# Expert parts above 128 rows: held weights in two passes of 256 middle columns, with a row count per rank

## The chip, the cores and the metric

The kernel runs on one core of a Trainium2 chip. The metric is the device time of one execution in microseconds, from the first to the last instruction of the core. A profile of one execution shows, for every engine, when each instruction ran and what it waited for.

## What is computed

The kernel is one layer of a diffusion backbone on 2048 latent tokens of 1024 channels, after 256 context tokens: an input projection, two groups of scans, an output projection with a norm, a mixture of experts, and a second norm. The change is in the mixture of experts, which the reference computes so (cut):

```python
weights = g_val * jax.nn.softmax(e_val, axis=-1)      # top group, then the two best of its 8 experts
expert_id = g_idx * EXPERTS_PER_GROUP + e_idx          # 32 experts, 2 for each of 2048 tokens
...
def expert_block(args):
    xb, e = args
    hid = jax.nn.silu(xb @ w1[e]) * (xb @ w3[e])       # 1024 -> 512 middle columns
    return hid @ w2[e]                                 # 512 -> 1024
...
return jnp.zeros((T, D), y.dtype).at[sorted_tok].add(y_slots)
```

All numbers are float32. On TensorE each product of two float32 matrices is made of three products of parts in the single-pass type float32r: high by high, low by high, and high by low.

## The kernel before

The projection, the scans, the first norm and the routing come first. The routing writes, for each expert, a list of token rows and weights (`idxD`), and takes the expert that leads in tokens as the first. Then the experts go by rank (by falling number of tokens). A fixed table, `NFIX`, says how many blocks of 128 rows each rank has: 3 for the first, 2 for the next 13, 1 for the last 18, 47 blocks together. A loop at the end (over `otab`) takes what the table did not foresee. The ranks with several blocks alternate with those of one (`sched`).

An expert's weights come in 12 pieces of 512 KB: 8 of `w1` and `w3`, each two chunks of 128 input channels by 512 middle columns, and 4 of `w2`. SyncE's queue fetches them in the order `pieces`, `NRAW` ahead. `split` makes of each raw piece a high part on ScalarE (`whi`) and a low part on VectorE (`wlo`), in a ring of `NUP` places for the way up and `NDOWN` for the way down. `pump` issues the next splits wherever the ring allows it.

A block goes through these steps. `gather` loads its list and its token rows with an indirect DMA. `turn` transposes the rows on TensorE and splits them into `xh`, `xl`. `up` multiplies: the 128 turned tokens are the stationary operand, 512 columns of weights move, and the result `ph` has a token on each partition. `hidden` makes SiLU and product. `turn_hidden` transposes the result and splits it into `hh`, `hl`. `down` multiplies them with `w2` (24 matmuls of 512 columns), and `put` scales the result and adds it to the tokens' rows in memory with an indirect DMA. The heart of `up` and of `down`:

```python
pe.matmul(p, self.xh[:, k, :], wh[:, kk, :], start=k == 0, stop=False)
pe.matmul(p, self.xl[:, k, :], wh[:, kk, :], start=False, stop=False)
pe.matmul(p, self.xh[:, k, :], wl[:, kk, :], start=False, stop=k == KC - 1)
...
pe.matmul(p, self.hh[:, k, :], wh[:, nh, :], start=k == 0, stop=False)
```

The program's order is written out by hand: for block `t` four steps of `up` (`kp`), and between them the turning of block `t + 1`, the transposes of the hidden values of block `t - 1` (after step 0), its way down (after step 1), and the gather for block `t + 2`. Every engine works through its own instructions in this order.

Of the kernel before, what the change touches and what calls it, by code (L numbers as in the profile page):

```python
# [19 lines left out]
D = 1024  # L20
# [13 lines left out]
NFIX = [3] + [2] * 13 + [1] * 18  # L34
NSB = sum(NFIX)
NOV = 30
NRAW, NUP, NDOWN = 10, 9, 4
# [4 lines left out]
# a word for each block of columns: the k chunk at which the scan is stepped, the steps there and after the block, and the  # L42
# order of what follows it: e evacuation, f filler, a scan steps, l later
# [28 lines left out]
def hymba_kernel(ctx, tc, xT, ctxT, x, small, rows, ada_w, w_in, gate_w, w_out, router_w, w1, w3, w2, out):  # L72
# [12 lines left out]
    u2D = dram.tile([L + 128, D], F32, name="u2D")  # L85
    accD = dram.tile([L + 128, D], F32, name="accD")
    idxD = dram.tile([32 * L, 2], I32, name="idxD")
# [30 lines left out]
    # ---- constants of the channels: forget-gate floor, decay rate of the RG-LRU  # L118
# [9 lines left out]
    def channel_constants():  # L128
# [11 lines left out]
        # softplus(-lam) = max(-lam, 0) + log1p(y), y = exp(-|lam|); log1p(y) = 2 artanh(y / (2 + y))  # L140
# [17 lines left out]
    def level_masks():  # L158
        """Level b pairs tokens of one 2b-block that lie in different b-halves."""
# [23 lines left out]
    # fixed blocks of a rank, rank on partition  # L183
# [3 lines left out]
    for v in range(max(NFIX)):  # L187
        pool.tensor_scalar(nmore, ecol, float(sum(n > v for n in NFIX)), None, op0=ALU.is_lt)
        pool.tensor_add(nfix, nfix, nmore)
    tok = const.tile([128, NTILE, 2, 2], I32, name="tok")  # L190
# [5 lines left out]
    # the expert of the first block, that block's rows, the expert of every rank, and the rank of every expert  # L196
# [5 lines left out]
    # every slot starts as a row past the tokens with weight 0, so that a block may be part full  # L202
    blank = tmp.tile([128, 512], I32, name="blank", tag="macc", bufs=1)
    zi = blank[:, 0:256].rearrange("p (r o) -> p r o", o=2)
    pool.memset(zi, 0)
    pool.iota(zi[:, :, 0], pattern=[[1, 128]], base=L, channel_multiplier=0)
    zero = blank[:, 256:512].bitcast(F32)
    pool.memset(zero, 0.0)

    def init_tables():  # L210
        rows0 = zero[:, None, :].to_broadcast([128, 4, 256])
        for a in range(4):
            pool.dma_start(idxD.rearrange("(p a r) o -> a p (r o)", p=128, a=4)[a], zi.rearrange("p r o -> p (r o)"))
            # rows past the tokens, and those of the last tile: the first block is read before that is stored
            if a < 3:
                t, r0 = ((u2D, L), (accD, L), (u2D, 0))[a]
                pool.dma_start(t[r0:r0 + 128, :].rearrange("p (n c) -> p n c", n=4), rows0)
            yield
# [4 lines left out]
    # ---- adaLN: shift and scale of the first layer norm, channel on partition  # L223
# [25 lines left out]
    def fetch_u(p, bi, k, n, pl, tag, bufs):  # L249
        """Raw channels of n chunks from chunk k."""  # L250
# [18 lines left out]
    def mod_sum(n0, also=()):  # L269
        """Columns n0 .. n0 + 3 on TensorE; also: k chunks of columns 4 .. 7 for VectorE meanwhile."""  # L270
# [53 lines left out]
    def build_u(p, bi, raws):  # L324
        """u = x * (1 + scale) + shift, channel on partition, split in two float32r; block bi of pass p, a chunk a step."""
# [53 lines left out]
    # ---- HGRN2  # L379
# [4 lines left out]
    class Head:  # L384
        """Head h over the W columns of pass p, the context first in pass 0."""
# [45 lines left out]
        def run(self):  # L431
            """The scan, in steps: every yield lets a block of the projection onto TensorE."""
# [65 lines left out]
            def chain(d, U, order):  # L498
                """States before each chunk of order; the state after the last goes to S."""
# [54 lines left out]
    # ---- RG-LRU  # L554
# [3 lines left out]
    class Lru:  # L558
        """Channels 128 t of the RG-LRU over the W columns of pass p."""
# [34 lines left out]
        def steps(self):  # L594
            """From the gates to the states of the first direction; rr: tanh, then sqrt(1 - a * a)."""
# [46 lines left out]
        def close(self):  # L642
            """Steps after the gates of the output are there: the other direction, or its store for later."""
# [15 lines left out]
    # the projection in blocks of columns, with the scans of the head before between them  # L659
# [62 lines left out]
    # at the turn of a pass the first blocks of two units go before their second ones, so that u can be made meanwhile  # L722
# [15 lines left out]
    # w_out takes the place of u when that is used up  # L738
# [131 lines left out]
    # ---- output projection, first norm, router, dispatch  # L870
# [5 lines left out]
    def rstd_of(pl, var, n, scale, eng=dve):  # L876
        """1 / sqrt(var * scale + EPS), elementwise on [128, n]."""
# [5 lines left out]
    with ExitStack() as st:  # L883
# [147 lines left out]
        def top2(i):  # L1031
# [22 lines left out]
            # the experts of the other groups are out  # L1054
# [9 lines left out]
            # weights: g_val * softmax of the two logits about their maximum  # L1064
# [22 lines left out]
        def place(i):  # L1087
# [7 lines left out]
            dve.scalar_tensor_tensor(dest[:, i, :], ee, float(L), sl, op0=ALU.mult, op1=ALU.add)  # L1095
# [172 lines left out]
    with ExitStack() as st:  # L1268
# [17 lines left out]
        def fetch(e, n, q=sp):  # L1286
            raw = er.tile([128, 2, 512], F32, name="raw", tag="raw")
            q.dma_start(raw, piece_src(e, n))
            return raw
# [305 lines left out]
```

## Time and profile before

| what | value |
|---|---|
| median of 3 runs (lowest to highest) | 2313.64 us (2311.78 to 2314.38) |
| the profiled execution: span of its instructions | 2313.6 us |
| first expert matmul to the end of the last way down | 1388.9 to 2238 us |
| busy in the span: TensorE, VectorE, ScalarE | 2125.5, 1758.1, 1165.0 us |
| moved by DMA | 446.01 MB |

The span of the profiled execution is its own time, and it agrees with the median. The busy time of TensorE is a sum of spans in which some matmul is under way; matmuls overlap, so the rate of a run of matmuls is read from their starts.

### The profile page before, as it was taken

To read this page: it belongs to the slowest core of one execution; us is meant where nothing else is said; L and a number is where in the kernel's file an instruction comes from. 1 tells how busy PE (TensorE), PEld (TensorE's weight loads), DVE (VectorE), ACT (ScalarE), POOL (GpSimd) and SP (SyncE) were. 2 spreads that over 40 slices of the span, in tenths; PEclk is the share of its full clock that TensorE was granted. 3 is DMA by queue.
4 is the path that set the end of the run, shared out by engine and by line. 5 is a ranking of instruction groups with operands and counts; after the bars stand their busy time and mean duration, and the time that the engine had idled before them with its cause. 6 is when DMAs were issued, how large, how long until landed. Compare 5 with 4: busy or idle time off the path is not lost.

```text
span 2313.6 us, 31918 instructions
## 1 busy us (share of the span) xinstructions
PE 2125.5 (92%) x11192; PEld 1824.8 (79%) x11192; DVE 1758.1 (76%) x2611; ACT 1165.0 (50%) x1807; POOL 609.4 (26%) x495
## 2 busy tenths in 40 slices
PE   7999999999999999996989969999999999999970
PEld 3788788999988988995777757888888888888850
DVE  5677776776776898896888975777777777777959
ACT  3446554654554654553333314555555555555733
POOL 4222233223233130002555551111111111111116
PEclk9999999999999999997999979999999999999985
DMA  8223243313424334328455228899999999999965
GB/s 266 96 99 114 78 146 101 123 62 121 136 77 139 101 107 139 126 95 293 148 172 171 88 80 292 285 298 299 302 299 299 301 298 289 288 295 294 355 194 242
DMA packets 213030, 446.01 MB, mean 193 GB/s; under 512 B 27635, under 2 KB 69619, under 8 KB 212356
## 3 DMA queue, kind: packets, MB, share of 16 engines
q1 hardware_dynamic: 186276, 378.37, 47.4%
q0 software_dynamic: 16784, 58.24, 10.2%
q10 hardware_dynamic: 9808, 7.34, 1.0%
q8 instruction: 89, 1.46, 0.3%
q14 instruction: 73, 0.60, 0.1%
HBM read 361.00 MB, written 82.89 MB: 192 GB/s over the span
## 4 chain that ended last, share of the span: by engine, by line
PE 64%; DVE 15%; issue 10%; DMA 5%; ACT 4%; POOL 2%; SPq 0%; POOLq 0%; DVEq 0%; ACTq 0%
PE ph L1337 7%; PE ph L1339 7%; PE ph L1338 7%; PE pp L349 7%; PE pp L351 7%; PE pp L350 7%; PE pye L1361 4%; PE pye L1363 4%; PE pye L1362 4%; PE pa L467 3%; PE pg L591 2%; DVE fr L987 2%; PE ptx L1325 2%; DMA raw<-in_w_dram 1%; POOL ur L340 1%
## 5 line engine op out<-in xcount | busy, mean ns | idle before, releaser
L1296 DVE TENSOR_TENSOR wlo<-raw,whi 128x1024 fp32r<-128x1024 f32 x384 | 455.2, 1222 | 81.9 <-ACT whi L1295 68.1
L349 PE MATMUL pp<-uh,wh 128*128 128x384 f32 (+2 forms) x1248 | 446.3, 358 | 4.6 <-ACT wh L239 2.4
L1295 ACT CAST whi<-raw 128x1024 fp32r<-128x1024 f32 x384 | 388.8, 1052 | 92.8 <-PE pye L1362 55.3
L350 PE MATMUL pp<-ul,wh 128*128 128x384 f32 (+2 forms) x1248 | 429.6, 344 | 4.8 <-DVE ul L240 4.8
L351 PE MATMUL pp<-uh,wl 128*128 128x384 f32 (+2 forms) x1248 | 428.6, 343 | 3.7 <-DVE wl L240 3.5
L1337 PE MATMUL ph<-whi,xh 128*128 128x512 f32 x752 | 309.1, 411 | 5.6 <-DMA raw<-in_w_dram 5.6
L1339 PE MATMUL ph<-wlo,xh 128*128 128x512 f32 x752 | 296.9, 395 | 2.2 <-DVE wlo L1296 2.2
L1338 PE MATMUL ph<-whi,xl 128*128 128x512 f32 x752 | 293.6, 390 | 0.0
L349 PEld LDWEIGHTS pp<-uh,wh 128*128 128x128 f32 x1248 | 239.4, 192 | 25.5 <-ACT rgs L592 5.2
L350 PEld LDWEIGHTS pp<-ul,wh 128*128 128x128 f32 x1248 | 239.0, 192 | 19.6 <-DVE ul L240 9.8
L351 PEld LDWEIGHTS pp<-uh,wl 128*128 128x128 f32 x1248 | 238.4, 191 | 13.9 <-DVE wl L240 4.9
L1308 POOL DMA_INDIRECT X<-u2D,ix x46 | 52.6, 1144 | 658.8 <-DMA ix<-idxD 565.8
L368 POOL TENSOR_SCALAR mraw<-mraw,sil 128x512 f32<-128x512 f32 x56 | 101.4, 1811 | 363.6 <-DMA mraw<-in_ada_w_dram 363.6
L1339 PEld LDWEIGHTS ph<-wlo,xh 128*128 128x128 f32 x752 | 141.6, 188 | 38.4 <-DVE wlo L1296 5.8
L1326 ACT CAST xh<-ptx 128x512 fp32r<-128x512 f32 x92 | 53.9, 586 | 226.3 <-PE ptx L1325 176.9
L1337 PEld LDWEIGHTS ph<-whi,xh 128*128 128x128 f32 x752 | 142.1, 189 | 30.3 <-ACT whi L1295 6.6
L1338 PEld LDWEIGHTS ph<-whi,xl 128*128 128x128 f32 x752 | 142.3, 189 | 25.8
L1361 PE MATMUL pye<-whi,hh 128*128 128x512 f32 x376 | 148.1, 394 | 0.7 <-ACT hh L1352 0.7
L1363 PE MATMUL pye<-wlo,hh 128*128 128x512 f32 x376 | 147.4, 392 | 0.0
L1362 PE MATMUL pye<-whi,hl 128*128 128x512 f32 x376 | 146.1, 389 | 0.2 <-DVE hl L1353 0.2
L467 PE MATMUL pa<-Q,km 128*128 128x128 f32 x896 | 124.9, 289 | 17.7 <-DVE Q L470 14.4
L240 DVE TENSOR_TENSOR wl<-wr,wh 128x1024 fp32r<-128x1024 f32 x84 | 108.5, 1292 | 39.1 <-ACT wh L239 39.1
(337 smaller groups left out, 4126.3 us busy)
## 6 DMA issues: line engine op xcount, KB each, us to landing
raw<-in_w_dram SPq DMA_DIRECT2D x384, 512.0 KB
wr<-in_w_in_dram SPq DMA_DIRECT2D x84, 512.0 KB
mraw<-in_ada_w_dram SPq DMA_DIRECT2D x64, 256.0 KB
aw<-in_ada_w_dram SPq DMA_DIRECT2D x16, 512.0 KB
fx<-in_x_dram SPq DMA_DIRECT2D x16, 512.0 KB
accD<-fr SPq DMA_DIRECT2D x16, 512.0 KB
u2D<-fu SPq DMA_DIRECT2D x16, 512.0 KB
f<-accD SPq DMA_DIRECT2D x16, 512.0 KB
```

The costliest lines, as they stand in the source:

```text
L349: pe.matmul(ps, wh[:, k, :], uh[:, k, :], start=k == 0, stop=False)
L350: pe.matmul(ps, wh[:, k, :], ul[:, k, :], start=False, stop=False)
L351: pe.matmul(ps, wl[:, k, :], uh[:, k, :], start=False, stop=k == KC - 1)
L467: pe.matmul(pa[:, c, :], km[:, s:s + 128], cut(Q, s, [(2 * b, 64 // b), (T + b, 2), (1, b)]), start=True, stop=True)
L1295: act.copy(hi, raw)
L1296: dve.tensor_sub(lo, raw, hi.bitcast(F32))
L1337: pe.matmul(p, self.xh[:, k, :], wh[:, kk, :], start=k == 0, stop=False)
L1338: pe.matmul(p, self.xl[:, k, :], wh[:, kk, :], start=False, stop=False)
L1339: pe.matmul(p, self.xh[:, k, :], wl[:, kk, :], start=False, stop=k == KC - 1)
L1361: pe.matmul(p, self.hh[:, k, :], wh[:, nh, :], start=k == 0, stop=False)
L1362: pe.matmul(p, self.hl[:, k, :], wh[:, nh, :], start=False, stop=False)
L1363: pe.matmul(p, self.hh[:, k, :], wl[:, nh, :], start=False, stop=k == 3)
```

## The change

Ranks get their own number of rows, `ROWS` (288 for the first, 224, 176, 160, 144 for the other thirteen above 128, then 128 down to 80), 4416 rows instead of 47 times 128 = 6016. The first 128 rows of the first rank stay one part; its other 160 and each of the other 13 ranks above 128 become one part of the new class `Wide`; the 18 ranks up to 128 are one part of the class `Block` with as many rows as the table says. That makes 19 `Block` and 14 `Wide` parts.

`w1` and `w3` are laid out in the input by halves of 256 middle columns, so a piece holds four chunks of input channels by 256 columns. Both classes make their way up in two passes, one for each half (steps 0 and 1, then 2 and 3), and `hidden` runs after each pass. In `Block` the tokens stay the stationary operand, and 256 columns move. In `Wide` the weights are held: 128 middle columns are stationary, the part's turned rows, high and low side by side, move (2n columns), then the low weights meet the high rows (n columns). Its result has a middle column on each partition, so nothing is transposed ahead of the way down; the two halves of the sum are added in `hidden`. The way down of a `Wide` part is made in two runs of 24 matmuls, one for each half of its rows: the first right after its last step of `up`, the second after the last step of the next part. The raw pieces ahead go from 10 to 8.

```diff
-NFIX = [3] + [2] * 13 + [1] * 18
+ROWS = [288] + [224] * 4 + [176] * 3 + [160] * 2 + [144] * 4 + [128] * 6 + [112] * 2 + [96] + [80] * 9
-NRAW, NUP, NDOWN = 10, 9, 4
+NRAW, NUP, NDOWN = 8, 9, 4
...
             def up(self, s):
                 h, n = s // 2, self.n
...
                 for kk in range(4):
                     k = 4 * (s % 2) + kk
                     for g in range(2):
                         wh, wl = self.w[2 * s + g]
+                        p = self.ps[:n, h, 256 * g:256 * g + 256]
...
+        class Wide:
...
+            def up(self, s, kk):
+                h, n = s // 2, self.n
+                k = 4 * (s % 2) + kk
...
+                for fb in range(2):
+                    f = slice(128 * fb, 128 * fb + 128)
+                    for g in range(2):
+                        wh, wl = self.w[2 * s + g]
+                        p = self.ps[g][:, fb, :]
+                        pe.matmul(p[:, :2 * n], wh[:, kk, f], self.x[:, k].rearrange("p h t -> p (h t)"), start=k == 0, stop=False)
+                        pe.matmul(p[:, :n], wl[:, kk, f], self.x[:, k, 0, :], start=False, stop=k == KC - 1)
+            def hidden(self, h):
...
+                for g in range(2):
+                    act.copy(t[:, g], self.ps[g][:, :, n:2 * n])
+                    dve.tensor_add(t[:, g], t[:, g], self.ps[g][:, :, :n])
+                act.activation(t[:, 0], t[:, 0], AF.Silu)
+                dve.tensor_mul(t[:, 0], t[:, 0], t[:, 1])
+                split_rows(self.hh[:, 2 * h:2 * h + 2, :], self.hl[:, 2 * h:2 * h + 2, :], t[:, 0])
+            def down(self, k, part):
...
+                s = slice(self.m * part, self.m * part + self.m)
+                down(self.hh[:, k, s], self.hl[:, k, s], self.w[8 + k], k, self.py, self.m)
...
+                    if s_ == 1 and t and not wide[t - 1]:
+                        finish(t - 1, 0)
+                    if s_ == 3 and t and wide[t - 1]:
+                        finish(t - 1, 1)
+                    if s_ == 3 and wide[t]:
+                        finish(t, 0)
...
+    pieces = lambda a: a.reshape(32, 2, 4, 128, 2, 256).transpose(0, 4, 1, 3, 2, 5).reshape(32, 4, 128, 1024)
```

The order of the built programs shows three places. The first is TensorE's work on one chunk of 128 input channels. Before, at the start of a block (`ph` is the result, `whi` and `wlo` the weights, `xh` and `xl` the turned tokens; the last figures are partitions by columns):

```order
L1337 MATMUL ph_12239<-whi_12078,xh_12174 128x512
L1338 MATMUL ph_12239<-whi_12078,xl_12175 128x512
L1339 MATMUL ph_12239<-wlo_12079,xh_12174 128x512
L1337 MATMUL ph_12240<-whi_12084,xh_12174 128x512
L1338 MATMUL ph_12240<-whi_12084,xl_12175 128x512
L1339 MATMUL ph_12240<-wlo_12085,xh_12174 128x512
```

Now, at the start of a `Wide` part of 224 rows, where `xw` holds the turned rows, high and low:

```order
L1439 MATMUL ph_12844<-xw_12639,whi_12578 128x448
L1440 MATMUL ph_12844<-xw_12639,wlo_12579 128x224
L1439 MATMUL ph_12845<-xw_12639,whi_12647 128x448
L1440 MATMUL ph_12845<-xw_12639,wlo_12648 128x224
L1439 MATMUL ph_12844<-xw_12639,whi_12578 128x448
```

Six matmuls of 512 columns for 128 rows and all middle columns have become eight, of 448 and 224 columns in turn, for 224 rows and half of the middle columns.

The second place is TensorE at the end of an expert's way up. Before, the last step of one block is followed by the next block's first step, and then by the transposes of the hidden values (`pth`):

```order
L1339 MATMUL ph_12113<-wlo_12157,xh_12072 128x512
L1325 MATMUL ptx_12207<-ident_87,X_12050 128x128 x4
L1337 MATMUL ph_12239<-whi_12078,xh_12174 128x512
...
L1339 MATMUL ph_12240<-wlo_12085,xh_12174 128x512
L1349 MATMUL pth_12253<-ident_87,hid_12214 128x128 x4
```

Now, at the end of a `Wide` part (`hw` holds its hidden values, split; `pye` is the result of the way down):

```order
L1439 MATMUL ph_13030<-xw_12639,whi_12943 128x448
L1440 MATMUL ph_13030<-xw_12639,wlo_12944 128x224
L1323 MATMUL pye_13152<-whi_12983,hw_12965 112x512
L1324 MATMUL pye_13152<-whi_12983,hw_12965 112x512
L1325 MATMUL pye_13152<-wlo_12984,hw_12965 112x512
L1323 MATMUL pye_13153<-whi_12983,hw_12965 112x512
```

The way down of the same part now stands directly behind its last step of `up`, with no other matmul in between.

The third place is VectorE between the two passes of such a part. Before, around the hidden product of a block:

```order
L1327 TENSOR_TENSOR xl<-ptx,xh 128x512
L1344 TENSOR_TENSOR hid<-hid,ph 128x512
L1296 TENSOR_TENSOR wlo<-raw,whi 128x1024 x2
L1353 TENSOR_TENSOR hl<-pth,hh 128x512
L1296 TENSOR_TENSOR wlo<-raw,whi 128x1024 x7
```

Now, for a part of 224 rows:

```order
L1297 TENSOR_TENSOR wlo<-raw,whi 128x1024 x4
L1332 SCALAR_TENSOR_TENSOR y<-pye,ix,g_12053 80x512 x2
L1297 TENSOR_TENSOR wlo<-raw,whi 128x1024
L1317 TENSOR_TENSOR hx<-pth,hx 128x2x80
L1317 TENSOR_TENSOR xx<-ptx,xx 128x4x80
L1297 TENSOR_TENSOR wlo<-raw,whi 128x1024 x3
L1450 TENSOR_TENSOR hidw<-hidw,ph 128x448 x2
L1452 TENSOR_TENSOR hidw<-hidw 128x448
L1317 TENSOR_TENSOR hw<-hidw,hw 128x448
L1297 TENSOR_TENSOR wlo<-raw,whi 128x1024 x4
```

A chain of two additions, a product and a split (`hidw`, `hw`) stands where one product stood, behind three splits of weights.

## Rows read from the trace of the kernel before

**Rows 1.** The page: span, and busy time of the engines

```profile
span 2313.6 us, 31918 instructions
PE 2125.5 (92%) x11192; PEld 1824.8 (79%) x11192; DVE 1758.1 (76%) x2611; ACT 1165.0 (50%) x1807; POOL 609.4 (26%) x495
```

**Rows 2.** Windows: length, PE, PEld, DVE, ACT, POOL busy, granted clock, DMA share, GB/s

```profile
1388.90:2231.00 842.10, 838.00 (x3930) 686.44 (x3930) 635.63 (x679) 481.74 (x569) 126.32 (x93) 1.00 0.91 297
1405.00:2200.00 795.00, 793.84 (x3753) 653.53 (x3752) 602.33 (x648) 456.54 (x542) 121.25 (x89) 1.00 0.92 299
```

**Rows 3.** Groups of instructions by line and form, 1388 to 2235 us

```profile
L1296 DVE TENSOR_TENSOR wlo<-raw,whi 128x1024 fp32r<-128x1024 f32 x384 | 455.2, 1222 | 81.9 <-ACT whi L1295 68.1 <-DMA raw<-in_w_dram 1.9
L1295 ACT CAST whi<-raw 128x1024 fp32r<-128x1024 f32 x384 | 388.8, 1052 | 92.8 <-PE pye L1362 55.3 <-DMA raw<-in_w_dram 32.4 <-DMA ix<-idxD 2.6
L1337 PE MATMUL ph<-whi,xh 128*128 128x512 f32 x752 | 309.1, 411 | 5.6 <-DMA raw<-in_w_dram 5.6
...
L1327 DVE TENSOR_TENSOR xl<-ptx,xh 128x512 fp32r<-128x512 f32 x92 | 63.4, 689 | 72.0 <-ACT xh L1326 58.9 <-issue 13.0
...
L1326 ACT CAST xh<-ptx 128x512 fp32r<-128x512 f32 x92 | 53.9, 586 | 226.3 <-PE ptx L1325 176.9 <-issue 49.4
...
L1349 PE MATMUL pth<-ident,hid 128*128 128x128 f32 x188 | 28.3, 273 | 2.0 <-DVE hid L1344 2.0
```

**Rows 4.** Timeline of TensorE: start, length, instruction; one way down

```profile
1648.22 0.39 PE L1361 MATMUL pye<-whi,hh 128*128 128x512 f32 x1
...
1653.71 0.39 PE L1337 MATMUL ph<-whi,xh 128*128 128x512 f32 x1
```

**Rows 5.** Waits, 1400 to 2225 us: total, times, longest; then SyncE's queue alone

```profile
ACT whi L1295 <- DMA raw<-in_w_dram: 26.0, 10, 3.3
...
SPq L1288 <- DVE wlo L1296: 519.7, 314, 15.8
```

**Rows 6.** DMA queues and issues, 1500 to 2000 us

```profile
q1 hardware_dynamic: 56015, 119.50, 67.2%
q0 software_dynamic: 7963, 29.02, 24.7%
...
raw<-in_w_dram SPq DMA_DIRECT2D x228, 512.0 KB
...
X<-u2D,ix POOLq DMA_INDIRECT x28, 6.9
```

**Rows 7.** Timeline of TensorE: float32r matmuls of 256 columns in the projection

```profile
108.63 0.28 PE L350 MATMUL pp<-ul,wh 128*128 128x256 f32 x1
...
109.83 0.28 PE L351 MATMUL pp<-uh,wl 128*128 128x256 f32 x1
```

**Rows 8.** Timeline of TensorE: two matmuls of 40 columns among those of 512

```profile
1136.69 0.31 PE L1029 MATMUL pl<-l2g,uT 128*128 128x40 f32 x2
...
1137.61 0.31 PE L1029 MATMUL pl<-l2g,uT 128*128 128x40 f32 x2
```

**Rows 9.** TensorE's plain float32: timeline of transposes and of 512 columns; group by form

```profile
1641.84 0.60 PE L1325 MATMUL ptx<-ident,X 128*128 128x128 f32 x4
...
173.22 3.59 PE L591 MATMUL pg<-xc,gw 128*128 128x512 f32 x8
...
L591 PE MATMUL pg<-xc,gw 128*128 128x512 f32 x32 | 14.5, 595 | 0.0
```

**Rows 10.** Start of the experts: timeline, and landing times of the first gathers

```profile
1388.94 0.79 PE L1337 MATMUL ph<-whi,xh 128*128 128x512 f32 x1 [5.63 <-DMA raw<-in_w_dram]
...
1391.96 0.97 POOL L1308 DMA_INDIRECT X<-u2D,ix  x1 [8.21 <-DMA ix<-idxD]
...
DMA to landing us min/median/max: 4.3/6.3/8.3
```

**Rows 11.** Windows around a wait of TensorE (columns as in Rows 2)

```profile
1336.00:1340.00 4.00, 1.14 (x4) 0.74 (x5) 2.82 (x7) 1.04 (x1) 0.00 (x0) 1.00 0.63 254
1340.00:1344.00 4.00, 4.00 (x16) 3.35 (x15) 3.69 (x17) 0.63 (x3) 2.70 (x4) 0.57 0.01 1
```

More of the change, by code (lines that the diff above doesn't have):

```diff
@@ L186, in hymba_kernel @@
     pool.memset(nfix, 0.0)
-    for v in range(max(NFIX)):
-        pool.tensor_scalar(nmore, ecol, float(sum(n > v for n in NFIX)), None, op0=ALU.is_lt)
+    below = 0
+    for v in sorted(set(ROWS)):
+        pool.tensor_scalar(nmore, ecol, float(sum(n >= v for n in ROWS)), float(v - below), op0=ALU.is_lt, op1=ALU.mult)
         pool.tensor_add(nfix, nfix, nmore)
+        below = v
     tok = const.tile([128, NTILE, 2, 2], I32, name="tok")
@@ new lines, in gather, with turned @@
+        def gather(row, n):
+            ix = ex.tile([128, 2], I32, name="ix", tag="ix", bufs=8)
+            sp.dma_start(ix[:n], idxD[bass.ds(row, n), :])
+            X = ex.tile([128, D], F32, name="X", tag="X", bufs=3)
+            pool.indirect_dma_start(out=X[:n], out_offset=None, in_=u2D, in_offset=bass.IndirectOffsetOnAxis(ap=ix[:n, 0:1], axis=0))
+            return ix, X
+        def turned(X, n, k0):
+            pt = psT.tile([128, 4, 128], F32, name="ptx", tag="pt")
+            for k in range(4):
+                pe.transpose(pt[:, k, :n], X[:n, 128 * (k0 + k):128 * (k0 + k) + 128], ident[:n, :n])
+            return pt[:, :, :n]
@@ L1373, in hymba_kernel @@
         SP = (mybir.EngineType.SP,)
         SPP = (mybir.EngineType.SP, mybir.EngineType.Pool)
[L1375 to L1376 removed]
+        many = [r for r in range(32) if ROWS[r] > 128]
+        one = [r for r in range(32) if ROWS[r] <= 128]
         sched = []
@@ L1386, in hymba_kernel @@
         for s_, r in enumerate(sched):
-            for j in range(NFIX[r]):
-                blocks.append((s_, j, j == NFIX[r] - 1))
+            o = 0 if s_ else 128
+            if o:
+                blocks.append((s_, 0, o, False))
+            blocks.append((s_, o, ROWS[r] - o, True))
         nb = len(blocks)
+        wide = [n > 128 for _, _, n, _ in blocks] + [False]
         def reg(s_):
@@ L1398, in hymba_kernel @@
         for t in range(nb + 1):
-            for kp in range(4):
-                pieces += [(blocks[t][0], 2 * kp + g) for g in range(2)] if t < nb else []
-                if kp == 1 and t:
-                    pieces += [(blocks[t - 1][0], n) for n in range(8, 12)]
+            ups = [(blocks[t][0], n) for n in range(8)] if t < nb else []
+            downs = [[(blocks[i][0], n) for n in range(8, 12)] if 0 <= i < nb and wide[i] == (i == t) else [] for i in (t - 1, t)]
+            pieces += ups[:4] + downs[0] + ups[4:] + downs[1]
         pieces = list(dict.fromkeys(pieces))
@@ L1427, in prepare, with finish, turn, used @@
                 if t < nb:
-                    s_, j, _ = blocks[t]
-                    B.append(Block(reg(s_) * L + 128 * j, weights[s_]))
+                    s_, o, n, _ = blocks[t]
+                    slot = "xw" if wide[t] or (not wide[t - 1] and B[t - 1].slot == "xs") else "xs"
+                    B.append((Wide if wide[t] else Block)(reg(s_) * LE + o, n, weights[s_], slot))
                     B[t].gather()
-            def finish(t):
+            def finish(t, part):
                 for k in range(4):
-                    B[t].down(k)
-                    if blocks[t][2]:
+                    while 8 + k not in B[t].w:
+                        pump(1)
+                    B[t].down(k, part)
+                    if blocks[t][3] and part == B[t].parts - 1:
                         state["down"] += 1
                     pump(1)
-                B[t].put()
+                B[t].put(part)
+            def turn(t, i):
+                if t < nb and i < B[t].turns:
+                    B[t].turn(i)
+            def used(t, i):
+                if blocks[t][3]:
+                    state["up"] += 2
+            def late(t):
+                if t == nb // 2:
+                    sp.dma_start(l2b, rows[0:1, 4096 + 3 * D:4096 + 4 * D].to_broadcast([128, D]))
             fetch_to(2)
-            B.append(Block(reg(0) * L, weights[0]))
+            B.append(Block(reg(0) * LE, 128, weights[0], "xs"))
             prepare(1)
```

264 lines of the change are left out of this document (148 added, 116 removed).

## The prediction

> **What bounds the kernel now.** I read the page first, then windows, groups, timeline, waits and DMA. The page's span is 2313.6 us [rows 1], the profiled execution's own time; it lies within 0.1 us of the median of the runs, so every sum below is made against 2313.6. Of a time of this size I take 0.2% (4.6 us) as about what a measurement can tell from no change.
>
> From 1388.9 us, their first matmul, to 2231 us, where only the last way down is left, the experts run alone. TensorE is busy in 838.0 of these 842.1 us, and in 793.8 of the 795 from 1405 to 2200, at the full clock [rows 2]. Since busy time can hide slack, I check the rate: one way down, 24 matmuls of 512 columns, starts at 1648.22 and the next matmul behind it at 1653.71 [rows 4], so 0.2288 us a matmul, without a gap. The stage is TensorE's. Counting: 752 matmuls of each of three kinds on the way up [rows 3] are 2256, or 47 blocks of 48, and the ways down are 47 times 24. 3384 times 0.2288 us is 774 us; the transposes take most of the rest.
>
> Two others stand close. DMA is at a share of 0.92 [rows 2]; yet ScalarE waited for raw weights 26 us in all, while SyncE's queue waited 519.7 us for VectorE to free a raw place [rows 5], so the supply is ahead of the demand. VectorE is busy 635.6 us of 842 [rows 2]. What TensorE gives up, these two can take over only so far.
>
> **TensorE, the Block parts.** 19 parts make 96 matmuls of 256 columns instead of 48 of 512. In the projection ten such matmuls, of the same type and each with its own stationary operand, take from 108.63 to 109.83 us [rows 7]: 0.120 us each. So 96 x 0.120 = 11.52 us against 48 x 0.2288 = 10.98 us, and 19 parts cost 10.2 us more. Fewer rows change nothing here, since rows are the stationary side.
>
> **TensorE, the Wide parts.** They replace 28 blocks: 28 x 48 x 0.2288 = 307.5 us. Each part is 64 pairs of one matmul of 2n columns and one of n. The wide one lies between rows: 0.120 us at 256 and 0.2288 at 512 make 0.425 ns a column, so 0.202 us at 448, 0.161 at 352, 0.147 at 320, 0.134 at 288. The narrow one, 144 to 224 columns in float32r, is in no row. The same line gives 0.106 to 0.072 us. But matmuls of 40 columns do not follow it: from 1136.69 to 1137.61 us there are two of them and three of 512 [rows 8], and 0.92 - 3 x 0.2288 leaves 0.117 us for each, so a new stationary operand seems to set a floor. Four transposes of 128 columns take 0.60 us with a last one of 0.27, so 0.110 us each [rows 3, 9]. I take 0.113 us, between these two, for every narrow matmul. A pair then takes 0.260 us (n = 160, 3 parts), 0.315 (224, 4 parts), 0.274 (176, 3 parts) and 0.247 (144, 4 parts); times 64, the 14 parts take 50.0 + 80.5 + 52.6 + 63.1 = 246.2 us. That is 61.3 us less.
>
> The two ends: with the line alone the 14 parts take 222.4 us, 24 less. At the rate of plain float32, which takes two times the time of float32r at 512 columns ((3.59 - 0.595) / 7 = 0.428 us [rows 9]) and 0.110 us at 128, a narrow matmul takes 0.123 to 0.190 us, and the parts 280 us, 33 more.
>
> **TensorE, the rest.** The ways down are 24 matmuls for each of 19 Block parts and 28 halves, 47 as before: no difference. The turning of rows is still 46 times 8 transposes. The 14 Wide parts need no transposes of hidden values: 28 x 4 x 0.110 = 12.3 us less [rows 3, 9].
>
> Sum on TensorE: +10.2 - 61.3 - 12.3 = -63.4 us.
>
> **A new wait.** The first way down of a Wide part stands right behind its last step of `up`. Its first two chunks use the first pass's hidden values, and give 12 x 0.2288 = 2.75 us of cover; the third needs the second pass's. That chain is copy, addition, SiLU (beside the other addition), product, cast, subtraction. By form ScalarE takes 0.586 us for 512 elements and 1.052 for 1024, VectorE 0.689 and 1.222 [rows 3], so at 2n = 448 about 0.53 and 0.62, at 288 about 0.38 and 0.46. Two of ScalarE and four of VectorE are 3.5 and 2.6 us, and some 0.4 us of handing over comes on top, against a cover of 2.97 us to the first use of the low part: a wait of 0.9 us at n = 224, none at 144. VectorE has three splits of weights (3.7 us) ahead of the chain, which begin when the step before ends and so run beside a step of 16 x 0.247 = 3.9 us or more. I take 0.7 us for each of 14 parts, 10 us; from below it is nothing, from above two late splits, 2.4 us more each. Behind the waiting matmul stand the rest of that way down and the next part's way up; the place of `pye` is taken again only two steps later, so nobody else waits.
>
> **The start.** The second part now turns its rows after the first step of the first part, no longer after the third. Its gather is issued at 1391.96 us and lands 4.3 to 8.3 us later [rows 10], about 1399, where the first step ends near 1394.5. But the weights for steps 2 and 3 also arrive late there, so most of this is hidden; SyncE's queue also reads the table of ranks before the third raw piece. Together I take 3 us; the ends are 0 and 6.
>
> **Edits at nothing.** VectorE: fewer turned rows, smaller hidden products in Block, 28 chains of four in Wide; by the same two forms its work grows some 10 us to 646 of about 800, so it stays behind TensorE's time. ScalarE grows 6 us. DMA: 228 raw pieces took 67.2% of 500 us, 1.47 us each, and 28 gathers with 28 additions 24.7%, 17 ns a row [rows 6]; 384 x 1.47 + 2 x 4416 x 0.0172 = 718 us, against 773 before, so the share stays at 0.9. If DMA had no slack, its 718 us would still be below 800. Eight raw pieces ahead instead of ten: the last five parts, of 128 rows, need 22.1 us of DMA and 18.3 of TensorE each, 19 us short together, and 8 raw pieces with some 7 split ones are 22 us of lead; gone, this costs up to 5 us. The larger lists, the zero fills and twelve small instructions of GpSimd at the start lie where it idles. No extra loop at the end: the routing of these inputs gives 275, 221, 221, 216, 214, 174 rows and so on, none above its place in `ROWS`.
>
> **Sum.** -63.4 + 10 + 3 = -50.4 us: 2313.6 - 50.4 = **2263 us**.
>
> **Rivals.**
>
> Narrow matmuls follow the line (no floor). For it: 256 columns fit no floor above 0.120 us. Against it: the 0.117 us at 40 columns. Then 24 us less: 2239 us. The Trainium skill (TensorE: Matmul & The Clock Gate, Back-to-back issue gap) gives about 81 ns for sustained pairs of weight load and matmul at 128 columns. By it the narrow ones would lie near the line, and the time near 2240 us; the rows at 40 and 128 columns, 0.117 and 0.110 us, do not agree, though both are plain float32.
>
> Narrow matmuls fall to the rate of plain float32. For it: no row shows float32r under 256 columns at the single-pass rate. Against it: nothing in the rows ties the rate to the width. Then 2263 + 33 = 2296 us.
>
> The Trainium skill (FP8 and Floating Point Precision, TensorE Precision Notes) counts four passes for true float32. Were a narrow matmul to take four times the columns' time, the parts would, as an estimate from that page, take about 425 us and the kernel 2442 us; the trace shows two times, not four, at 512 columns.
>
> The new wait decides (slower). Place: the third chunk of each Wide part's first way down. If the chain is held by two splits, TensorE waits 3.1 us. After a stretch in which it was busy 1.14 of 4 us, the granted clock of the next 4 us was 0.57, that is mostly the lower level [rows 11]; the 12 matmuls left then cost about 0.43 us instead of 0.23, 2.4 us more. 14 x 5.5 = 77 us in the place of 10: 2330 us. Against it: the splits' raw pieces were rarely late [rows 5]. It decides from (63.4 - 3) / 14 = 4.3 us a part on.
>
> Nothing gained: the supply of weights, at 0.92 of DMA's share, or VectorE's queue takes TensorE's place as the bound at once, near 2305 to 2315 us. Against it: the 718 and 646 us above.
>
> **How the numbers follow.** Forecast 0.48 (its own range 2250 to 2276: the ends of the wait and the start), no floor 0.17, plain rate 0.15, wait 0.11, nothing gained 0.05, four times 0.04. Below 2232 us lies little of the first rival; above 2304 lie the last three. So 2232 to 2304 us. Faster by over 0.2%: the first three cases, 0.80; same 0.05; slower 0.15, the wait and the four times.
>
> **What the profile of the changed kernel would show.** Right: starts in a run of Wide matmuls that give 0.31 us a pair at n = 224 and 0.25 at 144; 0.12 us for 256 columns; the third chunk of 14 ways down waiting under 1.5 us for VectorE; the stretch from the first expert matmul to the last way down near 792 us with TensorE busy almost throughout, DMA near 0.9. Wrong: pairs at 0.21 us for n = 144 (no floor) or at 0.39 for n = 224 (plain rate), waits of 3 us with a granted clock below 1 inside the stage, or TensorE waiting for raw weights.

## The result

The changed kernel takes 2282.31 us (median of 4 runs, 2275.72 to 2285.49), the kernel before 2312.71 (4 runs, 2310.96 to 2314.38): a ratio of 0.9865, 95% interval 0.9849 to 0.9882. It is 30 us faster where 50 were forecast, inside the range. The direction and the main saving were right. The time lies outside the 2250 to 2276 us that the prediction gave the forecast case itself, and that the number came out near is in part luck. The runs below show two errors of opposite sign: TensorE's own work shrank by more than the sum said, and a wait that the sum did not contain, with the lower clock behind it, gave back more than that. A second such wait stood hidden behind the first.

The page of the changed kernel: TensorE's busy time fell by 65 us, from 2125.5 [rows 1], its span by only 29.9. In the group of the first Block matmul, the figure behind the second bar is the idle time of TensorE just before it, then what ended it.

```profile
span 2283.7 us, 34562 instructions
...
PE 2060.1 (90%) x12440; PEld 1816.3 (80%) x12440; DVE 1757.6 (77%) x2703; ACT 1172.5 (51%) x1901; POOL 661.4 (29%) x507
...
L1377 PE MATMUL ph<-whi,xx 128*80 128x256 f32 (+3 forms) x608 | 179.8, 296 | 35.1 <-DVE hid L1386 31.3
```

Windows of it, with the columns of [rows 2]: the middle of the stage, then two pairs of 4 us, each pair before and behind a moment at which TensorE resumes after a wait, and last the 4 us behind two more waits, of 2.68 and 1.82 us.

```profile
1410.00:2150.00 740.00, 704.47 (x4717) 614.46 (x4716) 577.26 (x705) 440.33 (x601) 163.51 (x86) 0.99 0.89 286
...
1497.27:1501.27 4.00, 2.53 (x23) 2.32 (x21) 4.00 (x7) 3.68 (x5) 1.48 (x1) 1.00 1.01 367
1501.27:1505.27 4.00, 3.64 (x32) 3.42 (x32) 1.94 (x3) 0.80 (x3) 0.00 (x0) 1.00 1.01 275
...
2058.50:2062.50 4.00, 1.18 (x12) 1.03 (x10) 4.00 (x7) 2.44 (x4) 2.70 (x1) 1.00 1.02 414
2062.50:2066.50 4.00, 4.00 (x21) 4.00 (x21) 1.45 (x2) 0.00 (x0) 1.52 (x1) 0.57 1.04 396
...
1961.93:1965.93 4.00, 4.00 (x36) 4.00 (x37) 1.84 (x4) 0.65 (x2) 1.52 (x1) 1.00 1.04 401
...
2112.92:2116.92 4.00, 4.00 (x22) 4.00 (x23) 1.08 (x1) 0.00 (x0) 0.97 (x1) 0.61 1.02 325
```

TensorE, almost without a gap before [rows 2], now idles for 35.5 of 740 us. Behind the wait of 1.5 us at 1501 the granted clock stays at 1.00; behind that of 2.8 us at 2062 it is 0.57 for 4 us, mostly the lower level, which costs another 1.7 us (0.43 x 4). The length of the wait alone does not decide this: behind 2.68 us at 1961 the clock stays at 1.00, and behind 1.82 us at 2112 it is 0.61. DMA's share, 0.89, and VectorE, 577 of 740 us, are no bound. The waits of TensorE from 1400 to 2180 us (total, times, longest) name the place:

```profile
PE ph L1377 <- DVE hid L1386: 31.3, 15, 3.9
...
PE ptx L1312 <- DMA X<-u2D,ix: 3.1, 2, 1.6
PE pye L1323 <- ACT hw L1316: 1.9, 4, 0.6
...
PE pye L1324 <- DVE hw L1317: 0.7, 4, 0.2
```

The rows of `pye` are the wait that was forecast, 2.6 us of idle time in all; the starts of the matmuls show more of it (below). The first row was in no step. This wait stands in each of the 14 Block parts behind a Wide part, and in the first part, as in these rows of the timeline, ScalarE's first, then VectorE's, then TensorE's:

```profile
1499.45 0.38 ACT L1385 ACTIVATE hid<-ph 80x256 f32<-80x256 f32 x1 [0.32 <-PE ph L1379]
...
1498.54 2.35 DVE L1297 TENSOR_TENSOR wlo<-raw,whi 128x1024 fp32r<-128x1024 f32 x2
1500.81 0.41 DVE L1386 TENSOR_TENSOR hid<-hid,ph 80x256 f32<-80x256 f32 x1
...
1499.25 0.55 PE L1312 MATMUL ptx<-ident,X 112*128 112x112 f32 x4
1501.27 0.35 PE L1377 MATMUL ph<-whi,xx 128*80 128x256 f32 x1 [1.47 <-DVE hid L1386]
```

The SiLU of the first pass is done at 1499.83; VectorE is in two splits of weights, makes the product at 1500.81 to 1501.22, and only then does TensorE begin the second pass. That pass needs nothing of the product. But both passes write one tile `ph`, and its first matmul waits for the last reader of that tile, though the reader is in the other half. The built program shows the wait; below it the same instruction when the second pass has a tile of its own (first experiment):

```
L1377 MATMUL ph<-whi,xx 80x256 [waits DVE_49]
L1379 MATMUL ph<-whi,xx 80x256 [waits PE_49]
```

The sizes of the sum are seen in the timeline of TensorE. Its rows are, in this order: the first matmul of an expert; three Wide matmuls at n = 224; the first matmul of the first way down of a part of n = 224, the matmul right behind that way down, and another one 22 steps of 256 columns at 80 rows later; three pairs at n = 144 (first and last row); the first matmul of the first way down of a part of n = 144, its third chunk, and the matmul right behind it; a turning of four at 72 rows; seven steps of 256 columns at 128 rows (first and last row); the first matmul of the last way down.

```profile
1381.75 0.55 PE L1377 MATMUL ph<-whi,xx 128*128 128x256 f32 x1 [3.86 <-DMA raw<-in_w_dram]
...
1469.85 0.38 PE L1439 MATMUL ph<-xw,whi 128*128 128x448 f32 x1
1470.06 0.27 PE L1440 MATMUL ph<-xw,wlo 128*128 128x224 f32 x1
1470.16 0.37 PE L1439 MATMUL ph<-xw,whi 128*128 128x448 f32 x1
...
1487.09 0.40 PE L1323 MATMUL pye<-whi,hw 128*112 128x512 f32 x1
...
1493.38 0.28 PE L1377 MATMUL ph<-whi,xx 128*80 128x256 f32 x1
...
1495.89 0.28 PE L1378 MATMUL ph<-whi,xx 128*80 128x256 f32 x1
...
2026.79 0.34 PE L1439 MATMUL ph<-xw,whi 128*128 128x288 f32 x1
...
2027.52 0.34 PE L1439 MATMUL ph<-xw,whi 128*128 128x288 f32 x1
...
2046.65 0.39 PE L1323 MATMUL pye<-whi,hw 128*72 128x512 f32 x1
...
2050.12 0.45 PE L1323 MATMUL pye<-whi,hw 128*72 128x512 f32 x1 [0.52 <-ACT hw L1316]
...
2053.23 0.28 PE L1377 MATMUL ph<-whi,xx 128*128 128x256 f32 x1
...
2056.09 0.42 PE L1312 MATMUL ptx<-ident,X 72*128 72x72 f32 x4
...
2131.73 0.28 PE L1377 MATMUL ph<-whi,xx 128*128 128x256 f32 x1
...
2132.57 0.28 PE L1378 MATMUL ph<-whi,xx 128*128 128x256 f32 x1
...
2203.43 0.48 PE L1323 MATMUL pye<-whi,hx 128*128 128x512 f32 x1
```

Starts of 1469.85 and 1470.16 make 0.31 us a pair at n = 224, three pairs in 0.73 us make 0.243 at n = 144, and seven steps in 0.84 us make 0.120: the forecast 0.315, 0.247 and 0.120. At 80 rows, 22 steps in 2.51 us make 0.114. The stretch from the first matmul to the start of the last way down is 821.7 us, not 792.

### The profile page after: what moved, and what is told of

Same layout as the page of the kernel before. It is cut to its first block, busy times and chain, and to the rows that moved or that the text cites. A ratio compares the mean times of both kernels' runs of the same rounds, so it can differ in the third digit from the quotient of the medians.

```text
span 2283.7 us, 34562 instructions
## 1 busy us (share of the span) xinstructions
PE 2060.1 (90%) x12440; PEld 1816.3 (80%) x12440; DVE 1757.6 (77%) x2703; ACT 1172.5 (51%) x1901; POOL 661.4 (29%) x507
## 4 chain that ended last, share of the span: by engine, by line
PE 52%; DVE 19%; issue 13%; DMA 8%; ACT 5%; POOL 2%; SPq 0%; POOLq 0%; DVEq 0%; ACTq 0%
PE pp L354 7%; PE pp L356 7%; PE pp L355 7%; PE ph L1439 6%; DVE wlo L1297 3%; PE pa L472 3%; PE pye L1324 2%; DMA raw<-in_w_dram 2%; PE pye L1323 2%; PE ph L1440 2%; PE pye L1325 2%; PE pg L596 2%; PE ph L1377 2%; DVE fr L992 2%; PE ph L1379 2%
## 5 line engine op out<-in xcount | busy, mean ns | idle before, releaser
L1439 PE MATMUL ph<-xw,whi 128*128 128x448 f32 (+3 forms) x896 | 249.7, 355 | 0.7 <-DVE hid L1386 0.7
L1440 PE MATMUL ph<-xw,wlo 128*128 128x224 f32 (+3 forms) x896 | 217.9, 243 | 0.0
L1377 PE MATMUL ph<-whi,xx 128*80 128x256 f32 (+3 forms) x608 | 179.8, 296 | 35.1 <-DVE hid L1386 31.3
L1333 POOL DMA_INDIRECT accD<-y,ix x46 | 105.4, 2291 | 331.0 <-DVE y L1332 312.7
L1379 PE MATMUL ph<-wlo,xx 128*80 128x256 f32 (+3 forms) x608 | 176.1, 290 | 0.6 <-DVE wlo L1297 0.6
L1378 PE MATMUL ph<-whi,xx 128*80 128x256 f32 (+3 forms) x608 | 175.8, 289 | 0.0
L1439 PEld LDWEIGHTS ph<-xw,whi 128*128 128x128 f32 x896 | 168.1, 188 | 6.4 <-DVE hid L1386 0.9
L1440 PEld LDWEIGHTS ph<-xw,wlo 128*128 128x128 f32 x896 | 170.9, 191 | 1.2
L1306 POOL DMA_INDIRECT X<-u2D,ix x46 | 67.0, 1457 | 328.1 <-DMA ix<-idxD 187.9
L1377 PEld LDWEIGHTS ph<-whi,xx 128*80 128x80 f32 (+3 forms) x608 | 107.6, 177 | 39.3 <-DVE hid L1386 33.9
L472 PE MATMUL pa<-Q,km 128*128 128x128 f32 x896 | 125.0, 289 | 15.1 <-DVE Q L475 10.8
L472 PEld LDWEIGHTS pa<-Q,km 128*128 128x128 f32 x896 | 119.6, 195 | 20.5 <-ACT km L462 7.1
```

Source lines behind the costliest of these rows:

```text
L472: pe.matmul(pa[:, c, :], km[:, s:s + 128], cut(Q, s, [(2 * b, 64 // b), (T + b, 2), (1, b)]), start=True, stop=True)
L1377: pe.matmul(p, self.xh[:, k, :], wh[:, kk, :], start=k + g == 0, stop=False, skip_group_check=True)
L1439: pe.matmul(p[:, :2 * n], wh[:, kk, f], self.x[:, k].rearrange("p h t -> p (h t)"), start=k == 0, stop=False)
L1440: pe.matmul(p[:, :n], wl[:, kk, f], self.x[:, k, 0, :], start=False, stop=k == KC - 1)
```

## The experiments

Theory: the missing time is the wait of the second pass of a Block part, through the shared tile, and the lower clock behind it. Rivals: the supply of weights or VectorE's queue is the bound by now; or matmuls are slower than taken.

**A tile of its own for the second pass** (the readers of `self.ps` follow).

```
-                if s == 0:
-                    self.ps = psH.tile([128, 2, 512], F32, name="ph", tag="ph")
+                if s == 0:
+                    self.ps = {}
+                if s % 2 == 0:
+                    self.ps[h] = psH.tile([128, 2, 512], F32, name="ph", tag="ph")
```

> The second pass of a Block part gets a PSUM tile of its own; nothing else is changed. Theory (the missing gain is the wait of the second pass for VectorE's product, because both passes are halves of one tile): the 31.3 us before the first matmul of the second pass go, together with most of the lower clock behind them (about 1.6 us behind each of the six longest); 0 to 2 us of wait come back at the transposes of the hidden values. About 2245 us, between 2238 and 2252. Rival (VectorE's queue or the supply of weights is the limit, and the wait only shows where it ends): the idle time moves to another matmul, and the time falls by less than 10 us, to 2272 or more.

2264.49 us, ratio 0.9784 (0.9768 to 0.9800). The wait for the product is gone, so the tile was its cause, but only 18 us came of it. In its waits from 1400 to 2180 us another row leads:

```profile
PE ptx L1312 <- DMA X<-u2D,ix: 21.9, 8, 5.1
```

The timeline of SyncE's queue, GpSimd and TensorE before one such wait:

```profile
1699.08 0.34 SPq L1304 DMA_DIRECT2D ix<-idxD  x1
...
1708.41 1.31 POOL L1306 DMA_INDIRECT X<-u2D,ix  x1 [9.26 <-PE pye L1325]
...
1716.59 0.47 PE L1312 MATMUL ptx<-ident,X 80*128 80x80 f32 x4 [3.96 <-DMA X<-u2D,ix]
```

The window behind it:

```profile
1716.60:1720.60 4.00, 4.00 (x20) 4.00 (x21) 2.59 (x3) 3.27 (x4) 0.00 (x0) 0.57 0.64 161
```

A second wait stood behind the first: for the rows of the next Block part. Their list `ix` is issued at 1699.08 behind raw weights in SyncE's queue, the gather starts at 1708.41, and TensorE gets the rows at 1716.59, with the clock at 0.57 behind it. (The gather's row names a matmul as what came last before it; that the list held it is shown by the run with tile and list ahead, below, where these waits are gone.) Neither the theory's number nor the rival's "less than 10" held: the idle time moved, but to the gathers, not to weights or VectorE.

**The splits behind the product**, with the shared tile.

```
                     if s_ % 2:
                         B[t].hidden(s_ // 2)
+                    if s_ == 1 and hold:
+                        pump(2)
...
-                    pump(2)
+                    hold = not wide[t] and t and wide[t - 1]
+                    if s_ or not hold:
+                        pump(2)
```

> The shared tile stays, and so the wait; the two splits of weights that stand ahead of VectorE's product in a Block part behind a Wide part are issued behind it. Theory (the wait lasts as long as VectorE's queue holds the product): the product comes 1 to 2 us sooner in each of 15 parts, the wait falls from 31.3 us to 8 to 15, the time to about 2258 us (2252 to 2266). Rival (the second pass waits for something other than the product, or the splits are needed at once): no change, 2278 to 2286 us.

2261.75 us, 0.9770 (0.9757 to 0.9784), as the theory said. Its row of the waits:

```profile
PE ph L1377 <- DVE hid L1386: 13.1, 15, 3.2
```

**No Wide parts.**

```
-            blocks.append((s_, o, ROWS[r] - o, True))
+            m = ROWS[r] - o
+            if m > 128:
+                blocks.append((s_, o, m // 2, False))
+                o, m = o + m // 2, m // 2
+            blocks.append((s_, o, m, True))
```

> Every Wide part is replaced by two Block parts of half its rows: the new weight layout, two passes and row counts stay, the held weights go. Theory (the gain is that of the Wide parts, and a matmul of 256 columns costs half of one of 512): 28 blocks of 96 matmuls at 0.114 us are 61 us more than the 14 Wide parts, and their transposes 10 us more, but the 31 us of wait and the lower clock behind it go, since a way down stands between the passes of a Block part behind a Block part: 2305 to 2313 us. Rival (the gain came from fewer rows or the layout): well below 2300 us. With 0.120 us for 256 columns, as in the forecast: about 2335 us.

2328.84 us, 1.0059 (1.0044 to 1.0075). Without Wide parts the change is a loss, so they carry all of the gain: 0.9865 against 1.0059 is 45 us. The range was missed by 16 us. Rows come late here too, which it did not contain, and that is 15.1 us of waits (1400 to 2200 us):

```profile
PE ptx L1312 <- DMA X<-u2D,ix: 15.1, 14, 2.4
```

**Half of the columns of each narrow matmul.**

```
-                        pe.matmul(p[:, :n], wl[:, kk, f], self.x[:, k, 0, :], start=False, stop=k == KC - 1)
+                        pe.matmul(p[:, :n // 2], wl[:, kk, f], self.x[:, k, 0, :n // 2], start=False, stop=k == KC - 1)
```

> The narrow matmul of each pair takes half its columns (72 to 112 in the place of 144 to 224); the low part of the weights is left out for the other half of the rows. Floor of about 0.11 us for any narrow matmul: a pair keeps its 0.314 us at n = 224 and 0.244 at 144, and the time stays within 5 us of 2282. By columns alone (0.425 ns each): 64 x 1240 columns less, 34 us less, 2248 us.

2279.55 us, 0.9852 (0.9834 to 0.9871). The timeline at n = 224, where the narrow matmuls now have 112 columns:

```profile
1459.70 0.42 PE L1439 MATMUL ph<-xw,whi 128*128 128x448 f32 x1
...
1460.64 0.42 PE L1439 MATMUL ph<-xw,whi 128*128 128x448 f32 x1
```

Three pairs in 0.94 us: 0.313 each, as with 224 columns. The floor is shown, and the whole time agrees: 3 us less, where columns alone would make it 34. By the Trainium skill (TensorE: Matmul & The Clock Gate, Back-to-back issue gap) sustained pairs of weight load and matmul at 128 columns need about 81 ns; no run here agrees, a narrow matmul adds 0.11 us to its pair.

**The list of rows one part ahead**, with the shared tile (12 buffers for the lists in the place of 8).

```
-                        if t:
-                            prepare(t + 2)
+                        if t:
+                            if t + 2 < nb:
+                                B[t + 2].gather()
+                            prepare(t + 3)
```

`prepare` now issues the list alone.

> The changed kernel, whose list of rows (ix) is now fetched one part earlier than the gather (X) that needs it; the shared tile stays. Theory (with the shared tile the gathers come in time; they become late only when TensorE is faster): only the short waits for X near the start and the end go, 0 to 5 us: 2277 to 2283 us. Rival (late lists and gathers hold the changed kernel back as well): more than 10 us faster than 2282.

2269.61 us, 0.9805 (0.9791 to 0.9818): the rival held. TensorE's wait for the product fell from 31.3 to 21.5 us, and the timeline of ScalarE shows how: before a Block part of 128 rows, in the changed kernel and then here.

```profile
2055.86 1.05 ACT L1296 CAST whi<-raw 128x1024 fp32r<-128x1024 f32 x1 [1.99 <-DMA raw<-in_w_dram]
```

```profile
2046.44 0.40 ACT L1318 CAST xw<-ptx 128x288 fp32r<-128x288 f32 x1 [1.53 <-PE ptx L1314]
```

In the changed kernel weights come 2 us late at this place, and VectorE's splits ahead of the product with them; here they do not. That a late gather takes DMA's time from weights that are due fits these rows, and no run shows it by itself. One speaks against late weights as the whole cause: with the later turning alone (below) ScalarE waits 2.6 us for raw weights from 1400 to 2150 us, where it waits 10.8 in the changed kernel, and the wait for the product is still 30.9 us. What shortened that wait here stays open.

**The tile of its own and the list ahead.**

> A tile of its own for the second pass, and the list of rows one part ahead. Theory (in the run with its own tile alone, 22 of the 26 us in which TensorE waited for X arose because the list lands 9 us and more behind its issue, queued behind raw weights, and the gather starts that much later): these waits go, and the lower clock behind the longest of them: 20 to 30 us less than that run's 2264.5, 2235 to 2245 us. Rival (the supply of weights or VectorE's queue is the limit by now): the idle time moves again, 2257 us or more.

2242.83 us, 0.9692 (0.9679 to 0.9706), as the theory said.

**The same with the splits behind the product and a later first turning.**

> As the run before, with the two splits of weights issued behind VectorE's product, and the first turning of rows one step later in the first part. Theory: with the tile of its own nobody waits for the product any more, so the order of the splits gives nothing, and the start gives 2 to 4 us: 2232 to 2243 us, 1 to 5 us below the run before. Rival (the later splits make weights late): slower than the run before by 3 us or more.

2260.96 us, 0.9764 (0.9750 to 0.9777): 18 us worse, on the rival's side, though not by late weights. The splits now stand ahead of the subtraction of the turned rows (`xw`), whose PSUM tile the next turning needs:

```profile
PE ptx L1314 <- DVE xw L1319: 12.4, 13, 1.0
```

What saved time with the shared tile costs time without it; these waits are 12.4 of the 18 us, and the rest is open. The later first turning gave nothing: TensorE waits there for weights instead.

**The kernel before again.**

> The kernel before, unchanged, for a second profile. In the first one the first matmul of an expert starts at 1388.94 us, in the four profiles of changed kernels between 1380.6 and 1382.4. If the change shortens the part ahead of the experts, this profile shows 1388 to 1390 again; if that difference is one between executions, it shows 1383 or less.

2313.47 us. Its timeline has the first matmul of an expert at

```profile
1383.08 0.79 PE L1337 MATMUL ph<-whi,xh 128*128 128x512 f32 x1 [5.18 <-ACT whi L1295]
```

in the place of 1388.94 [rows 10], while its span, 2311.7 us, is only 1.9 below that of [rows 1]. So the start of the stage differs by 6 us between executions of one kernel (the last matmul of the routing's counts starts at 1373.74 us here, and at 1373.74 in the changed kernel too); the earlier start in the changed kernel is no gain of the change, and a cost of 3 us there can't be told. From the first matmul to the start of the last way down this execution takes 846.0 us (1383.08 to 2229.03), the changed kernel 821.7: of the 28 us between their spans 24 lie in that stretch.

**The tile of its own, and Block rows turned as late as before.**

```
-                    elif s_ % 2 == 0:
-                        turn(t + 1, s_ // 2)
+                    elif s_ > 1:
+                        turn(t + 1, s_ - 2)
```

> The tile of its own as in the first run, and the rows of a Block part turned behind the third and fourth step of the part ahead of it, as in the kernel before, no longer behind the first and third; the list of rows is fetched as late as ever. Theory (the waits for X come from asking for the rows two steps sooner, not from a list that is late in itself): the 20 us of waits for X in the middle of the stage go, 2235 to 2250 us, as in the run with the list one part ahead (2242.8). Rival (only an earlier list helps, since late gathers also take DMA time from weights that are due): 2257 us or more.

2232.72 us, 0.9657 (0.9643 to 0.9671), 2 us below the theory's range: the fastest kernel of this study, 48 us below the changed one (0.9865 - 0.9657, times 2313). The window, and then the longest waits of TensorE's matmuls from 1400 to 2140 us:

```profile
1410.00:2150.00 740.00, 738.27 (x5049) 650.71 (x5049) 618.97 (x753) 474.47 (x643) 178.31 (x90) 1.00 0.93 308
```

```profile
PE ph L1381 <- DVE wlo L1297: 0.8, 2, 0.4
PE pye L1324 <- DVE hw L1317: 0.7, 4, 0.2
```

TensorE is busy in 738.3 of 740 us at full clock. The waits for rows came from asking for them two steps sooner. The later turning also stands between the last step of a Wide part and its first way down, so it covers a part of the forecast wait.

**The later turning alone**, with the shared tile.

> The changed kernel with its shared tile, where only the rows of a Block part are turned behind the third and fourth step of the part ahead of it, as in the kernel before. Theory (two waits in one queue, the larger of which hides the smaller: the second pass still waits for the product, and the rows are then in time anyway): some 10 us less than 2282, as with the list one part ahead, 2266 to 2276 us, with 20 us or more still waited for the product. Rival (the early turning is the cause of both): the wait for the product falls under 10 us, and the time under 2255 us.

2277.41 us, 0.9848 (0.9830 to 0.9865), 4 us less than the changed kernel, a difference that the intervals do not separate, and 1 us outside the theory's range. Its other half held: TensorE still waits 30.9 us for the product. So the tile alone gives 18 us, the turning alone some 4 at most, both 48: each wait hid the other.

**All three: tile, turning, list ahead.**

> The tile of its own, the later turning, and the list of rows one part ahead. Theory (with the later turning no matmul in the middle of the stage waits for rows any more, and TensorE is the bound): the same time as with the first two, 2232.7 us, within 4 us. Rival (late lists still push gathers into the time of due weights): 2228 us or less.

2240.51 us, 0.9690 (0.9673 to 0.9707): neither; 8 us slower than without the earlier list, with no new wait in the middle of the stage. Its matmuls of 256 columns at 80 rows are slower, as its timeline shows (22 steps, first and last row).

```profile
1748.42 0.28 PE L1385 MATMUL ph<-whi,xx 128*80 128x256 f32 x1
...
1750.99 0.28 PE L1386 MATMUL ph<-wlo,xx 128*80 128x256 f32 x1
```

**The same with 16 buffers for the list.**

> The last run (own tile, later turning, list one part ahead) with 16 buffers for the list in the place of 12, nothing else. In the four kernels with 12 buffers a matmul of 256 columns at 80 rows takes 117 ns from start to start, in the kernels with 8 buffers 114; a buffer is 8 bytes a partition, so 12 move the tiles behind them by 32 bytes and 16 by 64. Theory (the place of the tiles in SBUF decides): 114 ns again, and the time falls by 5 to 9 us to 2231 to 2236. Rival (it is traffic or order of the earlier lists): 117 ns and 2238 us or more.

2237.68 us, 0.9674 (0.9661 to 0.9688). The same 22 steps:

```profile
1748.48 0.28 PE L1385 MATMUL ph<-whi,xx 128*80 128x256 f32 x1
...
1750.99 0.28 PE L1386 MATMUL ph<-wlo,xx 128*80 128x256 f32 x1
```

2.57 us for 22 is 117 ns, 2.51 is 114: the rate goes with the number of these buffers, and so the theory fits. In the built programs each takes 32 bytes of a partition and not 8, so the turned rows lie 128 bytes further with 12 than with 8, and 256 with 16 (the expectation counted 32 and 64), while the weights lie where they were. No run moves the tiles by another means. The time fell by 3 us, less than expected and inside the intervals; 3 ns in each of 9 x 96 matmuls would be 2.6. The rest of the 8 us stays open.

## Why the prediction was right, and where it was not

**Wide parts, -61.3 us: right.** The pairs have the forecast length, the floor is shown by halving the columns, and the run without Wide parts gives the whole gain back. The rivals "no floor", "plain rate" and "four times" are out.

**Block parts, +10.2 us: too high.** 256 columns take 0.120 us at 128 rows, but 0.114 at 80, so the step "fewer rows change nothing" failed. Why they are faster is not shown (in the run without Wide parts 72 rows take 0.118). With 9 parts of 80 rows, 7 of 128 and 3 between, it is about +4 (9 x 96 x 0.114 + 7 x 96 x 0.120 + 3 x 96 x 0.117, less 19 x 10.98).

**Transposes, -12.3 us: right for the hidden ones, but more was saved.** I left the turning of rows at no difference because their number is the same. Four transposes of 72 rows take 0.42 us where four of 128 take 0.60 [rows 9]; over 92 such turnings, with 93 rows on average, that is an estimated 9 to 10 us.

**The new wait, +10 us: right in sum, wrong in where.** TensorE's idle time there is 2.6 us, but matmuls overlap and the idle time hides most of it. By the starts (timeline above) the first way down takes 6.29 us at n = 224 and 6.58 at 144, where the second way down of the same part, which waits for nothing, takes 5.58 (1508.50 to 1514.08). Over the 14 parts that is 8.8 us. At 224 it is 0.7 us a part, 0.9 in the forecast; at 144 it is 0.9 to 1.0, where I expected none, and that the sum is near is luck. The timeline of VectorE in the changed kernel, first at 224, then at 144:

```profile
1487.53 1.15 DVE L1450 TENSOR_TENSOR hidw<-hidw,ph 128x448 f32<-128x448 f32 x2 [0.45 <-ACT hidw L1449]
...
2044.79 3.48 DVE L1297 TENSOR_TENSOR wlo<-raw,whi 128x1024 fp32r<-128x1024 f32 x3
2048.19 0.81 DVE L1450 TENSOR_TENSOR hidw<-hidw,ph 128x288 f32<-128x288 f32 x2
```

At 224 the splits end before the last step does, and VectorE waits for ScalarE's copy; at 144 the chain waits for three splits. The forecast counted the splits as hidden beside the last step, which at 144 rows is the shorter one.

**The start, +3 us: nothing that can be told.** TensorE waits 4.7 us for these rows in the changed kernel, but the run that turned them a step later waited for weights there and gained nothing, and executions of one kernel differ there by 6 us. The step failed in its reach. I priced the earlier turning for the second part alone. It holds for every Block part behind a Wide part: the rows are asked for two steps sooner, while list and gather are issued as late as ever. With the shared tile the other wait hides this; without it, it is 22 us of TensorE's time from 1400 to 2180 us.

**Nobody else waits: wrong.** The search for new waits went through Wide parts only. A Block part's second pass writes the tile that the first pass's SiLU and product read. Behind a Wide part nothing but one turning stands between the passes, and VectorE has two splits ahead of the product: 31.3 us in 15 parts, with the lower clock behind six of them. With this a sign of being wrong came true, waits of 3 us with a granted clock below 1 inside the stage, at a place that I had not named. I took VectorE's total of 646 of 800 us as the answer; the total was right (577 of 740) and says nothing of when one product comes.

**"Nothing gained": the limit is not reached.** In the fastest run VectorE is busy 619 of 740 us and DMA at 0.93 (window above), and TensorE sets the pace.

Together: with both waits taken away the change is worth about 79 us ((1 - 0.9657) x 2313), 16 more than the 63.4 of the sum, from the Block parts (6) and the turning (9 to 10). By its starts the forecast wait still costs 4.6 us there, so some 5 us more were saved than these two explain; that stays open. The waits and the clock behind them took 48 back, where I had put 13. Of these 48, TensorE's idle time is 34 (35.5 against 1.7 in the same window). The lower clock is about 10: in the 4 us behind the waits that end at 1401, 1762, 1911, 2011, 2062 and 2112 us the granted clock is 0.50, 0.59, 0.67, 0.57, 0.57 and 0.61. The rest is in part the forecast wait, of which the later turning covers about half.

## What to carry to other kernels

Where one pass is cut in two, ask of each buffer who reads the first half while the second is written: two halves of one tile may make one wait. A step that is moved forward must be priced at every place where the loop does it, with the list and the transfer that feed it. Read what a wait costs from the starts of the matmuls: here the idle time showed 2.6 of 8.8 us. And repair waits together: each of two hid the other, and alone they gave 18 and at most some 4 us of 48.

## What the hardware showed that was not expected

At 80 rows a matmul of 256 columns took 117 ns with 12 small buffers ahead of the tokens' tiles in SBUF, and 114 with 8 or 16. These tiles then lie 128 and 256 bytes further than with 8; that their place is the cause is likely and not shown. A narrow matmul with its own stationary operand added an estimated 0.11 us (its pair less the wide matmul by the forecast's line) at 224, 144 and 112 columns alike. And a wait of 2.8 us on TensorE cost 1.7 us more through the granted clock, while behind one of 1.5 us the clock stayed full; but it also stayed full behind one of 2.68 us and fell behind one of 1.82, so the length alone does not tell.
